# One tick more in a state-space pipeline, one PSUM tile for its inputs and outputs, and weight splits kept in DRAM

## The chip, the cores and the metric

The kernel runs on one core of a Trainium2 chip. The metric is the device time of one execution in microseconds (us), shorter is better. TensorE is PE in the rows (PEld is its weight load), VectorE DVE, ScalarE ACT, GpSimd POOL; SyncE (SP) issues every DMA of this kernel, in program order.

## The reference, cut to what matters

One layer of a hybrid decoder on 2048 prompt tokens (with 16 meta tokens ahead of them) and 8 running sequences of 8 new tokens, model width 1024, all in float32.

```python
xn = rmsnorm(h, norm_gain)
proj = xn @ w_in                       # 1024 x 6144: u_s, z_s, u_p, z_p, gates
# SSM branch: 64 groups of 16 channels, 64 complex states each
s[t] = abar * s[t-1] + bbar @ u_s[t]   # complex recurrence over time
y = gelu(Re(c @ s) + d * u_s)
y_s = y * sigmoid(y @ w_glu + b_glu)
# pooling branch: causal means over windows of 2, 4, 8, 16, then a 256x256 mix
y_p = ((windowed means of u_p) - u_p) @ pool_mix * pool_scale
merged = g_s * ((y_s * silu(z_s)) @ w_branch_ssm) + g_p * ((y_p * silu(z_p)) @ w_branch_pool)
out = rmsnorm(h + merged @ w_out)      # and the new SSM states and pooling rows
```

## The kernel before, in words

Features lie on partitions, tokens on the free axis. Tokens are cut into 4 groups (`GROUPS`, g0 to g3, some 512 to 544 columns each). A **unit** is one 128-row block of one weight matrix (or of the pooling mix) for one group: `proj` runs 8 blocks of depth, and each product of float32 matrices is made of three matmuls (`mm3`, L123): high part of the weight by high part of the data (L128), by its low part (L130), and low part of the weight by the high part (L132). So each weight block is loaded as `raw` (L187), rounded by POOL to `wh` (`w_high`, L103), and its remainder `wl` is taken by DVE (`w_low`, L206). The list `units` fixes the order of all 339 units; PE works through them. In iteration i of the last loop (L1295) the kernel calls `w_high` for unit i+2, then what earlier units left behind (posts), then events, then the matmuls of unit i, and at their end `w_low` for unit i+2 and `w_load` up to five units ahead. Every engine runs its own instructions in the order of the program. `raw`, `wh` and `wl` have 3 buffers each.

The units `us` make the SSM's input `u_s` (8 blocks for each group), in the order g1, g0 at the start, g2 and g3 later; the same 8 weight blocks are loaded and split each time.

The recurrence itself runs for 64 SSM groups in 32 pairs, in two **rounds** over time (`ROUNDS`: 135 and 131 chunks of 8 tokens), as a software pipeline spread over other units by `spread`. In **tick** i the pipeline handles several pairs, each at another step (`EARLY`, `LATE`, L587): the EARLY steps are put into the program a quarter of a tick in, the LATE ones at its end, between matmuls of the unit. For pair q: `st_load` (tick q, LATE) loads the input `su` and a matrix `smb`; `st_x` (q+1, LATE) is the PE product into the PSUM tile `sx`; `st_turn_a` (q+2, EARLY) copies `sx` with ACT (L519, L520; in round 1 also L522, which takes the last columns to `xs`); `st_turn_v` (q+2, EARLY) multiplies `sx` with DVE (L528); `st_scan` (q+2, LATE) is the scan (L540); `st_swap` (q+3, EARLY; L546) and `st_rot` (q+3, LATE) turn it back; `st_state` (q+4, EARLY) makes the state tile `sS` on POOL (L569); `st_y` (q+4, LATE) multiplies on PE into the PSUM tile `sy`, with `su` (L577) and with `sS` (L578); `st_out` (q+5, EARLY) copies `sy` to `sY` with ACT (L582) and stores it to `ys` in DRAM. `sx` and `sy` are two PSUM tiles with one buffer each; `sS` and `sY` have one buffer.

Round 0 has 37 ticks in 34 units (39 to 72: the `brp`/`gp` units of g0, and the `us` units of g2 and g3), so seven units hold two ticks. Round 1 has 37 ticks between units 75 and 217, at most one in a unit.

At the start the weight blocks of units 0 and 1 are loaded and split before the loop (L1267 to L1283); then SP issues the load of block 2 (L1284), some constants, and the rows of x for g0. In iteration 0 POOL first rounds block 2 (L103) and then adds squares of x (`x_sq`, L720), as DVE does; ACT makes the squares in two temporaries, of which each is free again when its sum is done. DVE puts both sums together (L723), and at the start of unit 2 PE sums them over the partitions (L746).

The matrices of the recurrence are made in the background at the start (`batches`) and kept in DRAM in `mat_d`. PSUM tiles that are needed elsewhere: `acc` (2 x 512 columns, 3 buffers) for all units; `bx` and `by`, one half each, for two early sums of squares (`rms_sum`, L746). `rsqrt_mean` reads such a sum with ACT (L137) and then with DVE (L139), one half after the other, into separate columns of its SBUF tiles.

Of the kernel before, what the change touches and what calls it, by code (L numbers as in the profile page):

```python
# [20 lines left out]
P = 128  # L21
# [67 lines left out]
def hybrid_step(ctx, tc, a):  # L89
# [74 lines left out]
    mat_d = dram.tile([GRP, P, 3, P], F32, name="mat_d")  # L164
# [13 lines left out]
    def w_load(key, k=1):  # L178
        if key in raws or key in halves or key in splits:
            return  # L180
# [18 lines left out]
    def w_low(key, k=1):  # L199
# [146 lines left out]
    def batches(bg):  # L346
# [63 lines left out]

        def s5(b):
# [4 lines left out]
            SY.dma_start(mat_d[gs, :, 0].rearrange("g p m -> p g m"), btT)  # L416
            SY.dma_start(mat_d[gs, :, 2].rearrange("g p m -> p g m"), d["ct"].rearrange("p g c t -> p g (c t)"))
# [19 lines left out]
        def s10(b):  # L437
# [5 lines left out]
            SY.dma_start(mat_d[4 * b:4 * b + 4, :, 1].rearrange("g p m -> p g m"), mp)  # L443
# [34 lines left out]
    def st_load(g, q):  # L478
        x = stile("su", 4, g.kn + NS)
# [5 lines left out]
        SY.dma_start(mb, mat_d[two(q), :, 0].rearrange("q p m -> p q m"))  # L485
# [21 lines left out]
    def st_x(g, q):  # L507

        d = pr[q]
        d["px"] = sw["sx"][:, :, :g.kn]  # L510
# [3 lines left out]
    def st_turn_a(g, q):  # L514
# [6 lines left out]
        if g.last:  # L521
            A.activation(sw["xs"][:, two(q)], ps[:, :, kp:], AF.Copy)  # L522
# [20 lines left out]
    def st_swap(g, q):  # L543
# [16 lines left out]
    def st_state(g, q):  # L560
# [3 lines left out]
        s = stile("sS", 1, g.kn)  # L564
# [8 lines left out]
    def st_y(g, q):  # L573
        d = pr[q]
        d["py"] = sw["sy"][:, :, :g.kn]
        for j in range(2):
            PE.matmul(d["py"][:, j], d["m"][:, j, :P], d["u"][:, j], start=True, stop=False)  # L577
            PE.matmul(d["py"][:, j], d["m"][:, j, P:], d["S"][:, j], start=False, stop=True)  # L578
# [18 lines left out]
    def final_states():  # L597
        SY.dma_start(a["fin"], state)
# [815 lines left out]
```

## Time and profile before

| what | value |
|---|---|
| median of 3 runs | 2157.99 us (2157.77 to 2158.32) |
| the profiled execution's own time | 2159.06 us |
| its span | 2157.3 us |
| PE busy | 2086.0 us (97%) |
| DVE, POOL, ACT busy | 1395.2 (65%), 923.7 (43%), 686.8 us (32%) |
| mean granted TensorE clock | 0.989 of full speed |

The span is from the first to the last instruction of the program. Busy time is the time in which at least one instruction of the engine ran; matmuls overlap in the record, so the sum of their durations is more than the busy time. Idle time is put down to what released the engine.

### The profile page before, as it was taken

Reading aid. Unit: us, or ns where it says so; the run is one execution under the profiler, and the core shown is the slowest. Engines: PE = TensorE matmul, PEld = TensorE weight load, DVE = VectorE, ACT = ScalarE, POOL = GpSimd, SP = SyncE. Lnnn points to the kernel's source line nnn. Section 1 sums busy time; section 2 is a strip of 40 time slices with the busy share of each in tenths; the row PEclk is TensorE's granted clock in tenths of the full one; section 3 lists DMA queues with packets and bytes.
Section 4 is the critical chain, followed back from the end, with each engine's and each line's share of the span. In section 5 each row is a group of like instructions: output and inputs, shape, how many; then the busy total and the mean of one; then the engine's idle time right before and its main releaser. Section 6 shows DMA issues by size and latency. Waiting matters only on the chain.

```text
span 2157.3 us, 37693 instructions
## 1 busy us (share of the span) xinstructions
PE 2086.0 (97%) x14968; PEld 1970.9 (91%) x14968; DVE 1395.2 (65%) x1916; ACT 686.8 (32%) x1243; POOL 923.7 (43%) x1054
## 2 busy tenths in 40 slices
PE   7999999889899999999899999999999999999998
PEld 7988899888799999999899999999999987888887
DVE  7989968878656686644856676633633767456444
ACT  3213357645434332144544432121210221112101
POOL 3387747565444452233544452233421333244222
PEclk9999999999999999999999999999999999999999
DMA  6646556486944453244444543234333443343223
GB/s 199 145 117 165 164 169 200 144 202 155 183 127 124 151 144 120 89 121 137 120 125 144 157 139 125 82 119 118 104 100 109 144 128 120 101 133 117 91 97 105
DMA packets 261279, 287.77 MB, mean 133 GB/s; under 512 B 106096, under 2 KB 203760, under 8 KB 261104
## 3 DMA queue, kind: packets, MB, share of 16 engines
q1 hardware_dynamic: 261104, 285.37, 45.7%
q8 instruction: 118, 1.93, 0.4%
q14 instruction: 57, 0.47, 0.1%
HBM read 242.32 MB, written 40.62 MB: 131 GB/s over the span
## 4 chain that ended last, share of the span: by engine, by line
PE 71%; DVE 6%; DMA 4%; ACT 3%; issue 2%; POOL 2%; SPq 0%; DVEq 0%; ACTq 0%; POOLq 0%
PE acc L128 23%; PE acc L132 23%; PE acc L130 23%; DMA ys<-sY 1%; DVE wl L206 1%; DVE sX L537 1%; PE sy L578 1%; PE sx L512 1%; PE sy L577 1%; DVE sX L540 1%; DMA raw<-in_wb 1%; DVE al L114 1%; DVE sph L558 1%; DMA mat_d<-mp 1%; DVE sph L499 0%
## 5 line engine op out<-in xcount | busy, mean ns | idle before, releaser
L128 PE MATMUL acc<-ah,wh 128*128 128x268 f32 (+4 forms) x4504 | 1058.9, 305 | 8.9 <-ACT ah L705 6.6
L132 PE MATMUL acc<-ah,wl 128*128 128x268 f32 (+4 forms) x4504 | 1049.0, 302 | 3.7 <-DVE wl L206 3.7
L130 PE MATMUL acc<-al,wh 128*128 128x268 f32 (+4 forms) x4504 | 1047.9, 302 | 0.0
L103 POOL TENSOR_SCALAR wh<-raw 128x1024 fp32r<-128x1024 f32 (+1 forms) x336 | 392.5, 1168 | 969.9 <-PE acc L130 869.7
L128 PEld LDWEIGHTS acc<-ah,wh 128*128 128x128 f32 x4504 | 729.3, 190 | 44.2 <-issue 7.8
L132 PEld LDWEIGHTS acc<-ah,wl 128*128 128x128 f32 x4504 | 727.8, 189 | 32.0 <-DVE wl L206 4.7
L130 PEld LDWEIGHTS acc<-al,wh 128*128 128x128 f32 x4504 | 728.2, 190 | 27.0 <-DVE al L706 0.3
L206 DVE TENSOR_TENSOR wl<-raw,wh 128x1024 fp32r<-128x1024 f32 (+1 forms) x336 | 432.3, 1288 | 140.9 <-POOL wh L103 136.1
L896 ACT ACTIVATE sg<-acc,hb 128x536 f32<-128x536 f32 (+2 forms) x64 | 45.0, 702 | 402.2 <-PE acc L132 402.1
L528 DVE TENSOR_TENSOR sX<-sx,scc 128x270 f32<-128x270 f32 (+1 forms) x64 | 27.2, 424 | 107.3 <-ACT xs L522 65.0
L114 DVE TENSOR_TENSOR al<-H,ah 128x536 fp32r<-128x536 f32 (+3 forms) x96 | 89.3, 963 | 6.8 <-POOL ah L103 5.2
L952 DVE SCALAR_TENSOR_TENSOR H<-po,H 128x536 f32<-128x536 f32 (+2 forms) x32 | 23.8, 745 | 103.4 <-ACT po L950 103.4
L853 ACT ACTIVATE H<-acc 128x536 f32<-128x536 f32 (+2 forms) x64 | 39.1, 610 | 140.9 <-PE acc L132 140.7
L105 ACT ACTIVATE ah<-H 128x536 fp32r<-128x536 f32 (+3 forms) x80 | 50.8, 646 | 92.6 <-DVE H L884 77.1
L854 DVE SCALAR_TENSOR_TENSOR H<-H,acc 128x536 f32<-128x536 f32 (+2 forms) x64 | 44.8, 700 | 48.1 <-ACT H L853 47.6
L577 PE MATMUL sy<-su,smc 128*128 128x135 f32 (+1 forms) x256 | 52.2, 285 | 18.7 <-ACT sY L582 15.7
L820 DVE TENSOR_TENSOR w<-E 128x483 f32<-128x483 f32 (+2 forms) x32 | 21.9, 685 | 73.4 <-POOL E L807 58.0
L963 DVE SCALAR_TENSOR_TENSOR sg<-sg,acc 128x536 f32<-128x536 f32 (+2 forms) x32 | 22.4, 700 | 70.9 <-PE acc L132 70.9
L540 DVE TENSOR_TENSOR_SCAN sX<-r,state,sX 128x135 f32<-128x135 f32 (+1 forms) x128 | 65.7, 554 | 2.3
L950 ACT ACTIVATE po<-acc,hb 128x536 f32<-128x536 f32 (+2 forms) x32 | 22.5, 704 | 134.8 <-PE acc L132 134.8
L905 DVE SCALAR_TENSOR_TENSOR G<-sg,acc 128x536 f32<-128x536 f32 (+2 forms) x32 | 22.4, 699 | 64.9 <-PE acc L132 64.9
L578 PE MATMUL sy<-sS,smc 128*128 128x135 f32 (+1 forms) x256 | 53.1, 290 | 11.2 <-POOL sS L569 11.2
(232 smaller groups left out, 2227.8 us busy)
## 6 DMA issues: line engine op xcount, KB each, us to landing
raw<-in_wb SPq DMA_DIRECT2D x318, 512.0 KB, 3.8
smc<-mat_d SPq DMA_DIRECT2D x64, 256.0 KB, 4.1
smb<-mat_d SPq DMA_DIRECT2D x64, 128.0 KB, 3.3
xr<-in_xb SPq DMA_DIRECT2D x21, 268.0 KB, 4.4
H<-in_xb SPq DMA_DIRECT2D x19, 268.0 KB, 4.4
su<-us SPq DMA_DIRECT2D x32, 135.0 KB, 4.1
ys<-sY SPq DMA_DIRECT2D x32, 135.0 KB, 4.6
us<-po SPq DMA_DIRECT2D x16, 268.0 KB, 6.6
```

The costliest lines, as they stand in the source:

```text
L103: G.tensor_scalar(out, in_, 1.0, 0.0, ALU.mult, ALU.add)
L105: A.activation(out, in_, AF.Copy)
L114: V.tensor_tensor(l, x, h.bitcast(F32), ALU.subtract)
L128: PE.matmul(out, wh, xh, start=first, stop=False)
L130: PE.matmul(out, wh, xl, start=False, stop=False)
L132: PE.matmul(out, wl, xh, start=False, stop=last)
L206: V.tensor_tensor(l[:, c], r[:, c], h[:, c].bitcast(F32), ALU.subtract)
L540: V.tensor_tensor_scan(x[:, j], r8[:, i].to_broadcast([P, g.kp]), x[:, j], state[:, i], ALU.mult, ALU.add)
L577: PE.matmul(d["py"][:, j], d["m"][:, j, :P], d["u"][:, j], start=True, stop=False)
L578: PE.matmul(d["py"][:, j], d["m"][:, j, P:], d["S"][:, j], start=False, stop=True)
L854: V.scalar_tensor_tensor(self.v3(out), self.v3(out), 1.0, self.pv(ps), ALU.add, ALU.mult)
L896: A.activation(self.v3(s), self.pv(ps), AF.Tanh, scale=0.5, bias=hb[:, b, fb:fb + 1])
```

## The change

- **Weights.** When one of the 8 `us` weight blocks is split for the first time (for g1), its `wh` and `wl` are also stored to DRAM (`wu_d`, 2 x 512 KB). For g2 and g3 the units have kind "v": `w_high` then loads `wh` and `wl` from there, and nothing is loaded as `raw`, rounded or subtracted.
- **Pipeline.** `st_y` comes one tick later (offset 5), `st_out` at 6; the loading of its matrix becomes a step of its own at the end of EARLY (`st_mat`, offset 4). `sx` and `sy` become views of one PSUM tile `bk` of 2 x 512 columns: `sx` of even and odd pairs in the first 320 columns of the two halves, `sy` in columns 320 to 480 of both. `su` has 5 buffers, `sS` 3, and `st_out` writes its output into the pair's `sS`; `sY` is gone. `xs` goes pair by pair to DRAM and is read back in `final_states`. There are 38 ticks to a round.
- **Matrices.** `mat_d` is laid out by pairs, so that rows of the DMAs are twice as long.
- **Pooling.** The windowed sums of `up_post` run over flattened rows where they can, and the small copies of L822 are gone.

```diff
-    mat_d = dram.tile([GRP, P, 3, P], F32, name="mat_d")
+    mat_d = dram.tile([GRP // 2, P, 3, 2, P], F32, name="mat_d")
+    xs_d = dram.tile([P, GRP, NS], F32, name="xs_d")
...
+    wu_d = [dram.tile([P, 2, 1024], F32, name=f"wu{f}") for f in range(NB)]
...
     def w_load(key, k=1):
-        if key in raws or key in halves or key in splits:
+        if key in raws or key in halves or key in splits or key[0] == "v":
...
     def w_high(key, k=1):
...
+        if key[0] == "v":
+            hl = [wpool.tile([P, 1024], F32R, tag=t, bufs=3, name=t) for t in ("wh", "wl")]
+            for j in range(2):
+                SY.dma_start(hl[j].bitcast(F32), wu_d[key[1]][:, j])
+            splits[key] = hl
+            return
...
     def w_low(key, k=1):
...
+        if key[1] < NB and key[0] == "w" and key[1] not in stored:
+            stored.add(key[1])
+            for j, x in enumerate((h, l)):
+                SY.dma_start(wu_d[key[1]][:, j], x.bitcast(F32))
...
     def st_load(g, q):
-        x = stile("su", 4, g.kn + NS)
+        x = stile("su", 5, g.kn + NS)
...
-        SY.dma_start(mb, mat_d[two(q), :, 0].rearrange("q p m -> p q m"))
+        SY.dma_start(mb, mat_d[q, :, 0])
...
     def st_x(g, q):
-        d["px"] = sw["sx"][:, :, :g.kn]
+        d["px"] = sw["sx"][q % 2][:, :2 * g.kn].rearrange("p (q k) -> p q k", q=2)
...
     def st_turn_a(g, q):
         if g.last:
-            A.activation(sw["xs"][:, two(q)], ps[:, :, kp:], AF.Copy)
+            xs = stile("sxs", 2, NS)
+            A.activation(xs, ps[:, :, kp:], AF.Copy)
+            SY.dma_start(xs_d[:, two(q)], xs)
...
+    def st_mat(g, q):
+        d = pr[q]
         d["m"] = stile("smc", 2, 2 * P)
-        SY.dma_start(d["m"].rearrange("p q (j m) -> p q j m", j=2),
-                     mat_d[two(q), :, 1:3].rearrange("q p j m -> p q j m"))
+        SY.dma_start(d["m"], mat_d[q, :, 1:3].rearrange("p j q m -> p j (q m)"))
...
     def st_state(g, q):
-        s = stile("sS", 1, g.kn)
+        s = stile("sS", 3, g.kn)
...
     def st_out(g, q):
-        y = stile("sY", 1, g.kn)
-        A.activation(y, pr.pop(q)["py"], AF.Copy)
+        d = pr.pop(q)
+        y = d["S"]
+        A.activation(y, d["py"], AF.Copy)
         SY.dma_start(chans(g, ys_d, q), y)
...
-    EARLY = ((5, st_out), (3, st_swap), (2, st_turn_a), (1, st_sin), (4, st_state),
-             (0, st_phase), (2, st_turn_v), (2, st_turn_g))
-    LATE = ((3, st_rot), (0, st_wrap), (2, st_scan), (4, st_y), (1, st_x), (0, st_load))
-    NTICK = NPAIR + 5
+    EARLY = ((6, st_out), (3, st_swap), (2, st_turn_a), (1, st_sin), (4, st_state),
+             (0, st_phase), (2, st_turn_v), (2, st_turn_g), (4, st_mat))
+    LATE = ((3, st_rot), (0, st_wrap), (2, st_scan), (5, st_y), (1, st_x), (0, st_load))
+    NTICK = NPAIR + 6
...
     def up_post(self, fb, ps):
                 if d < T:
-                    V.tensor_tensor(nxt[:, d:], cur[:, d:], cur[:, :T - d], ALU.add)
                     V.tensor_tensor(nxt[:, :d, 1:], cur[:, :d, 1:], cur[:, T - d:, :ke - 1], ALU.add)
-                    V.tensor_copy(nxt[:, :d, 0:1], cur[:, :d, 0:1])
...
     def u_us(g, f, delay=2):
-        i = add("w", W_US + f, g.us, f)
+        i = add("v" if g.gi > 1 else "w", W_US + f, g.us, f)
...
     def to_ssm():
-        for n in ("sx", "sy"):
-            sw[n] = ps.tile([P, 2, 160], F32, name=n)
-        sw["xs"] = sw["p"].tile([P, GRP, NS], F32, name="xs")
+        bk = ps.tile([P, 2, 512], F32, name="bk")
+        sw["sx"] = [bk[:, j, :320] for j in range(2)]
+        sw["sy"] = bk[:, :, 320:480]
```

## Rows read from the trace of the kernel before

**Rows 1.** The page: busy time by engine.
```profile
PE 2086.0 (97%) x14968; PEld 1970.9 (91%) x14968; DVE 1395.2 (65%) x1916; ACT 686.8 (32%) x1243; POOL 923.7 (43%) x1054
```

**Rows 2.** Waits of PE over the span: us in total, times, longest.
```profile
PE sy L577 <- ACT sY L582: 15.7, 8, 3.3
PE sy L578 <- POOL sS L569: 11.2, 11, 1.7
PE sx L512 <- DVE sX L528: 10.4, 10, 2.2
PE sy L577 <- DMA smc<-mat_d: 2.9, 3, 1.3
```

**Rows 3.** Windows at the low clock: the last in the pipeline; sum of eight.
```profile
1275.70:1279.10 3.40, 3.40 (x18) 3.40 (x17) 3.05 (x6) 0.00 (x0) 2.25 (x3) 0.50 0.38 91
...
sum 40.80, PE 37.64 PEld 35.54 DVE 31.59 ACT 17.98 POOL 24.16; mean PE 4.71 PEld 4.44 DVE 3.95 ACT 2.25 POOL 3.02
```

**Rows 4.** Groups by line: busy us, mean ns | idle before, releasers.
```profile
L206 DVE TENSOR_TENSOR wl<-raw,wh 128x1024 fp32r<-128x1024 f32 (+1 forms) x336 | 432.3, 1288 | 140.9 <-POOL wh L103 136.1 <-DMA mt<-ks 4.3
...
L528 DVE TENSOR_TENSOR sX<-sx,scc 128x270 f32<-128x270 f32 (+1 forms) x64 | 27.2, 424 | 107.3 <-ACT xs L522 65.0 <-ACT sXw L520 42.3
...
L582 ACT ACTIVATE sY<-sy 128x270 f32<-128x270 f32 (+1 forms) x64 | 24.6, 384 | 36.9 <-DMA ys<-sY 35.1 <-PE sy L578 1.7
...
L822 DVE COPY w<-w 128x2 f32<-128x2 f32 (+1 forms) x40 | 7.4, 185 | 0.0
```

**Rows 5.** Timeline of all engines, one tick of round 1: start, us, instruction.
```profile
1270.61 0.40 PE L132 MATMUL acc<-ah,wl 128*128 128x268 f32 x2
...
1272.59 0.49 PE L577 MATMUL sy<-su,smc 128*128 128x131 f32 x2 [1.58 <-ACT sY L582]
...
1274.40 0.41 DVE L528 TENSOR_TENSOR sX<-sx,scc 128x246 f32<-128x246 f32 x1 [0.44 <-ACT xs L522]
...
1274.71 0.49 PE L578 MATMUL sy<-sS,smc 128*128 128x131 f32 x2 [1.63 <-POOL sS L569]
...
1275.49 0.86 PE L512 MATMUL sx<-su,smb 128*128 128x131 f32 x4
```

**Rows 6.** Timeline, the first tick in which L528 ends after PE's arrival.
```profile
343.43 0.39 PE L577 MATMUL sy<-su,smc 128*128 128x135 f32 x2
...
343.48 0.44 DVE L528 TENSOR_TENSOR sX<-sx,scc 128x270 f32<-128x270 f32 x1 [1.34 <-ACT sXw L520]
```

**Rows 7.** Timeline, ACT and DVE: halves of one PSUM tile read, of two tiles.
```profile
411.67 0.44 DVE L139 SCALAR_TENSOR_TENSOR sg<-acc,sg 128x268 f32<-128x268 f32 x1
...
412.14 0.48 ACT L137 ACTIVATE sg<-acc,epst 128x268 f32<-128x268 f32 x1 [0.98 <-DVE sg L139]
```
**Rows 8.** Timeline, the same lines where the halves are two tiles.
```profile
48.61 0.49 ACT L137 ACTIVATE sg<-by,epst 128x272 f32<-128x272 f32 x1
```

**Rows 9.** Timeline of the start.
```profile
8.20 0.33 SPq L187 DMA_DIRECT2D raw<-in_wb  x1
...
15.10 1.08 POOL L103 TENSOR_SCALAR wh<-raw 128x1024 fp32r<-128x1024 f32 x1 [3.04 <-DMA raw<-in_wb]
15.19 2.06 DVE L206 TENSOR_TENSOR wl<-raw,wh 128x1024 fp32r<-128x1024 f32 x1
...
20.48 1.34 POOL L720 TENSOR_TENSOR ss<-ss,w 128x536 f32<-128x536 f32 x1 [2.04 <-ACT w L719]
...
26.33 1.20 PE L746 MATMUL bx<-rs,onesm 128*128 128x268 f32 x2 [3.32 <-DVE rs L723]
```

**Rows 10.** DMA from 440 to 485 us: share of 16 engines; issues, median us to landing.
```profile
q1 hardware_dynamic: 12506, 9.44, 92.7%
...
raw<-in_wb SPq DMA_DIRECT2D x5, 512.0 KB, 5.4
...
ys<-sY SPq DMA_DIRECT2D x6, 135.0 KB, 5.9
```

**Rows 11.** DMA from 5 to 13 us, where large packets fill the engines.
```profile
DMA packets 1350, 2.85 MB, mean 356 GB/s; under 512 B 147, under 2 KB 248, under 8 KB 1350
```

More of the change, by code (lines that the diff above doesn't have):

```diff
@@ L172, in hybrid_step @@
     raws, halves, splits = {}, {}, {}
+    stored = set()
+    wu_d = [dram.tile([P, 2, 1024], F32, name=f"wu{f}") for f in range(NB)]
     def cut(n, k):
@@ L409, in s4, with mat_store @@
             d["ps"], d["pk"] = ps, pk
+        def mat_store(b, j, x):
+            SY.dma_start(mat_d[2 * b:2 * b + 2, :, j].rearrange("q p g m -> p q (g m)"),
+                         x.rearrange("p (q g) m -> p q (g m)", g=2))
         def s5(b):
@@ L415, in s5 @@
             A.activation(btT, d["ps"], AF.Copy)
-            SY.dma_start(mat_d[gs, :, 0].rearrange("g p m -> p g m"), btT)
-            SY.dma_start(mat_d[gs, :, 2].rearrange("g p m -> p g m"), d["ct"].rearrange("p g c t -> p g (c t)"))
+            mat_store(b, 0, btT)
+            mat_store(b, 2, d["ct"].rearrange("p g c t -> p g (c t)"))
             o = 4 * (b % 2)
@@ L442, in s10 @@
                          mt[:, o:o + 4].rearrange("p g (t c) -> p g c t", c=GCH), AF.Copy)
-            SY.dma_start(mat_d[4 * b:4 * b + 4, :, 1].rearrange("g p m -> p g m"), mp)
+            mat_store(b, 1, mp)
         S7 = [(7 + i, lambda b, i=i: s7(b, i)) for i in range(1, NPART)]
@@ L576, in st_y @@
         for j in range(2):
-            PE.matmul(d["py"][:, j], d["m"][:, j, :P], d["u"][:, j], start=True, stop=False)
-            PE.matmul(d["py"][:, j], d["m"][:, j, P:], d["S"][:, j], start=False, stop=True)
+            m = slice(j * P, (j + 1) * P)
+            PE.matmul(d["py"][:, j], d["m"][:, 0, m], d["u"][:, j], start=True, stop=False)
+            PE.matmul(d["py"][:, j], d["m"][:, 1, m], d["S"][:, j], start=False, stop=True)
     def st_out(g, q):
-        y = stile("sY", 1, g.kn)
-        A.activation(y, pr.pop(q)["py"], AF.Copy)
+        d = pr.pop(q)
+        y = d["S"]
+        A.activation(y, d["py"], AF.Copy)
         SY.dma_start(chans(g, ys_d, q), y)
-    EARLY = ((5, st_out), (3, st_swap), (2, st_turn_a), (1, st_sin), (4, st_state),
-             (0, st_phase), (2, st_turn_v), (2, st_turn_g))
-    LATE = ((3, st_rot), (0, st_wrap), (2, st_scan), (4, st_y), (1, st_x), (0, st_load))
-    NTICK = NPAIR + 5
+    EARLY = ((6, st_out), (3, st_swap), (2, st_turn_a), (1, st_sin), (4, st_state),
+             (0, st_phase), (2, st_turn_v), (2, st_turn_g), (4, st_mat))
+    LATE = ((3, st_rot), (0, st_wrap), (2, st_scan), (5, st_y), (1, st_x), (0, st_load))
+    NTICK = NPAIR + 6
     def tick(steps, g, i):
@@ L598, in final_states @@
         SY.dma_start(a["fin"], state)
+        xs, s0 = (tmp.tile([P, GRP, NS], F32, tag="po", bufs=2, name="s0") for _ in range(2))
+        SY.dma_start(xs, xs_d)
         for j in range(2):
-            s0 = tmp.tile([P, GRP, NS], F32, tag="po", bufs=2, name="s0")
             SY.dma_start(s0, a["s0"][:, j])
             G.tensor_tensor(s0, s0, a8[:, j].unsqueeze(2).to_broadcast([P, GRP, NS]), ALU.mult)
-            G.tensor_tensor(sw["xs"], sw["xs"], s0, ALU.add)
-        SY.dma_start(a["fins"], sw["xs"])
+            G.tensor_tensor(xs, xs, s0, ALU.add)
+        SY.dma_start(a["fins"], xs)
     mid = []
@@ L818, in up_post @@
                 nxt = self.t(tmp, f"w{step % 2}", 1, shape=[P, T, ke])
+                if d < 4:
+                    n, o, c = (x.rearrange("p t k -> p (t k)") for x in (nxt, cur, cur))
+                    i = d * ke + step
+                    V.tensor_tensor(n[:, i:], o[:, i:], c[:, step:T * ke - d * ke], ALU.add)
+                elif d < T:
+                    V.tensor_tensor(nxt[:, d:, 1:], cur[:, d:, 1:], cur[:, :T - d, 1:], ALU.add)
+                else:
+                    V.tensor_tensor(nxt[:, :, 2:], cur[:, :, 2:], cur[:, :, 1:ke - 1], ALU.add)
                 if d < T:
-                    V.tensor_tensor(nxt[:, d:], cur[:, d:], cur[:, :T - d], ALU.add)
                     V.tensor_tensor(nxt[:, :d, 1:], cur[:, :d, 1:], cur[:, T - d:, :ke - 1], ALU.add)
-                    V.tensor_copy(nxt[:, :d, 0:1], cur[:, :d, 0:1])
-                else:
-                    V.tensor_tensor(nxt[:, :, 1:], cur[:, :, 1:], cur[:, :, :ke - 1], ALU.add)
                 cur = nxt
```

## The prediction

> **What bounds the kernel now.** I read the page first. PE is busy in 97% of the span [rows 1], so the change can only be worth what lies in PE's waits, and what it adds to them. The list of PE's waits comes next, since it names what ended each. PE idles for 71 us in all (the span less its busy time), and 40 of these lie in the SSM pipeline [rows 2]: the product y waits for its PSUM tile to be copied out (15.7 us), for the state tile (11.2) and for its matrix (2.9), and the product x waits for DVE to have read `sx` (10.4). The rest lies at the start and in waits for DVE.
>
> Third, the granted clock. There are eight windows at half clock inside the span (1.2 GHz, the lower of the two levels), 40.8 us together [rows 3]. Two of 3.4 us belong to the first 130 us; the other six, 34 us, each follow a tick in which PE stood still for 2.8 us or more. At half clock half of that is lost: 17 us. So a pipeline without waits would give 40 + 17 = 57 us at most. That is what the change could win.
>
> Fourth, the groups by line, for who holds whom. ACT stood 35.1 us in `st_out` until the store of the pair before had left `sY` [rows 4]: that delays everything behind it on ACT, `st_swap` and `st_turn_a` too, and so the DVE multiplication L528. L528 itself waits for ACT, 65.0 us of it for L522. L522 reads other columns of `sx` and writes `xs`, which L528 doesn't touch; both only read. So in this program two engines don't read one PSUM tile at once, whatever the columns: the order of the program is kept by semaphores. The timeline of two sums of squares tells more. Where both halves lie in one `acc` tile, ACT's read of the second half starts at 412.14, 0.03 us after DVE's read of the first half (411.67 + 0.44), after a wait of 0.98 us [rows 7]; the same holds at 817, 1299 and 1742 us. Where the halves are two tiles, `bx` and `by`, it doesn't wait at all [rows 8]. So the waits go by tile, and not by half.
>
> **The pipeline, part by part.** What goes: `st_y` a tick later has its state tile ready, so PE's 11.2 us for POOL go. With `sY` gone, ACT no longer waits for the store in `st_out` (35.1 us of ACT). The wait moves to POOL: `sS` with 3 buffers comes free when that same store has landed, again a tick after its issue, so `st_state` waits in its place, and behind it on POOL `st_phase`, `st_turn_g` and the next rounding. That has a tick of slack before PE needs it, and I cost it at nothing; without the slack it is again the 11.2 us.
>
> What comes: `sx` and `sy` lie in one tile now. In the program of one tick the accesses are: `st_out` (ACT), `st_turn_a` (ACT), `st_turn_v` (DVE, L528), `st_y` and `st_x` (PE). By [rows 4, 7] `st_y` must therefore wait for L528 of the same tick, which it didn't before. Before, only `st_x` did, and the 8 instructions of `st_y` ran ahead of it (the last six of them take 0.78 us in [rows 5], so all 8 about 1 us). So two tiles for x buy nothing, since y stands in front of x in PE's order. A tick of round 1 shows it [rows 5]: PE is through with the unit at 1271.0, y starts at 1272.59 and goes on at 1274.71, x at 1275.49. L528 ends at 1274.81. Then y could begin only there: 3.8 us of waiting in place of 3.2.
>
> I go through all 64 ticks in this way. In 27 of them L528 ends after PE arrived at y; the first is that of [rows 6] (343.92 against 343.43), the last that of [rows 5]. The sum is 60.3 us, against 39.7 us of PE waits in the same ticks. From the 60.3 I take 10 us for ticks of round 0 in which ACT had waited for the store (where, instead, the scan of the tick before or DVE's own queue sets the end); 3.8 us and 2.2 us at the first waiting tick of round 1 and the last of round 0, where y and L528 no longer meet because of the tick more; and 2 us for ticks in which DVE was late and has 1.29 us less to do per `us` unit [rows 4]. I add 1.8 us, since the 38 ticks of round 1 fall on other units: three instead of two in the `zs` units of g1, where ACT is late. That is 60.3 - 10 - 3.8 - 2.2 - 2 + 1.8 = 44.1 us against 39.7: **+4.4 us**. The bounds: if y waits only for `st_out`, some 15 us remain (-25); if POOL's new wait is late for PE too, the 11.2 us come back, +16.
>
> The matrix load `st_mat` is issued as long before its product as it was, a tick and three quarters; on SP it now stands behind the store of `xs` (round 1), which waits for L522, 2 us of ACT after the `st_out` that it stood behind before. It has ticks of 12 us there: 0, at most the 2.9 us of [rows 2] once more.
>
> Clock: seven or eight ticks would have a wait of 2.8 us or more in one piece, against six windows now: **+2 us**, between -12 and +8.
>
> By the Trainium skill (PSUM — Partial Sum Buffer, "PSUM bank collisions raise a hardware error") two engines must be kept apart by bank, reads against reads included, and different banks may be used at the same time. By that rule the sum would be 6 us less, as in the second rival below. The trace agrees on reads against reads (L522 and L528), and not on the banks: the rows at 412 us hold back the other half of the tile too.
>
> **The weights.** For 16 units POOL loses a rounding and DVE a subtraction [rows 4]; neither holds PE in those units except as counted. In their place SP loads 1 MB a unit instead of 0.5 MB, after PE has left the slot of the unit before, with two units of time until it is needed. Behind that wait on SP stand the loads of x, the stores to `ys` and the loads of `su` of the same unit; none of them could be used before PE is there either, so the order costs nothing, only the bytes do. But from 440 to 485 us, in the `us` units of g2, the DMA engines are 92.7% busy, and a store of 135 KB takes 5.9 us to land [rows 10]. Large packets go at 356 GB/s when the engines are full [rows 11], so 512 KB cost 1.5 us of all engines, for 6 units of that stretch 9 us; the free share is 3.3 us, and the longer rows of `mat_d` give back something that no row prices. So up to 5 us don't fit there; in the units of g3 less, since the stretch is not full. I take **+5 us**, bounds 0 (the work slides into idle stretches beside it) and +18 (16 units by 1.5 us are 24 us, of which a quarter finds room).
>
> **The start.** Here is a term that I can follow exactly. Each first split now issues two stores from SP, in the place of `w_low`. For block 1 that lies ahead of the load of block 2, and waits for DVE's subtraction, which comes after all of `x_raw` and ends at 17.25 [rows 9]. Before, the load of block 2 was issued at 8.20 and POOL rounded it at 15.10. Now it is issued at about 17 (the subtraction a little faster without POOL beside it) and lands behind a 512 KB store: some 4.5 us later, at 21 to 22.5. POOL stands at the rounding until then, and its adds of squares stand behind it; ACT's squares wait for them in turn. From 22 on: rounding 1.1, three adds of 1.34 [rows 9] with two squares of 0.65 between them, DVE's sum 1.0 to 1.5: 29 to 31. PE's sum L746 starts there and not at 26.33. PE has nothing else: **+3.5 us**, bounds +2.5 and +6 (a longer stretch at the low clock). The stores hold their `wh` and `wl` until they have landed, but these slots are used again three units later. The other six pairs of stores fall on weights that are loaded three units ahead: 0.
>
> **The rest.** 72 small copies go, 7.4 us of DVE for the larger group [rows 4]. PE waits for DVE in two places of the pooling units of g0; I take **-1 us**, bounds 0 and -3. `final_states` now uses one tile for two loads in turn: SP stands there for some us longer, but PE does not wait at all there in this trace; 0, at most +3. The 32 small stores of `xs` cost SP a place behind ACT in round 1, where loads have more than a tick; 0.
>
> Sum: 4.4 + 2 + 5 + 3.5 - 1 = +13.9 us on 2159.06 us of the profiled execution, 2173.0 us. That execution was 1.07 us above the median, so I predict 2172 us.
>
> **Rivals.** What a measurement can tell from no change is 0.2%, 4.3 us.
> - *Faster, 2129 us.* Views of one tile are kept apart by what they touch. Then x has two places and y waits for `st_out` alone: 25 us of waits and 12 us of clock go, the start, the DMA and the copies keep 7.5. For it: the three largest waits of [rows 2] are those that the change addresses. Against it: L522 and L528, and the rows at 412 us. It decides if PE no longer waits for L528. 0.15.
> - *By halves, 2166 us* (2160 to 2172). y's half goes ahead of L528 where the pair's `sx` lies in the other half: every second one of some 25 waiting ticks, 12 by 0.5 us. For it: the halves are 512 columns each, as those of `acc`. Against it: [rows 7]. This is the page's rule. 0.14.
> - *The DMA engines become the bound, 2191 us.* 18 us in place of 5, and 8 us of clock in place of 2: PE waits for `su`, `smc` and x. For it: 92.7%. Against it: the stretches beside it have room. 0.15.
> - *Nothing, 2158 us.* ACT's 35 us had hidden more than I credit, and that just pays for the start. 0.06.
>
> My forecast (2162 to 2182) has 0.50. The range 2145 to 2192 leaves out nearly all of the first rival and a third of the third. Chances: faster 0.18 (the first rival, and half of the last), same 0.14 (the other half, the lower edge of the second rival and of my own case), slower 0.68.
>
> **What would show it.** Among PE's waits, that of L578 for POOL is gone, and the largest is y (L577) for DVE's L528, 35 to 45 us; there is none of x for L528. ACT's wait for the store is gone, POOL has one. L746 starts at 29 to 31 us. DMA landings in the `us` units grow to 6 to 8 us. If y starts while L528 still reads, the forecast is wrong; if L746 starts before 28, the start is.

## The result, and the profile after

The changed kernel takes 2188.89 us (median of 4 runs, 2185.74 to 2189.65) against 2158.15 us of the kernel before beside it: 1.0138 times as long (95% interval 1.0122 to 1.0154), 30.7 us more. The forecast was 2172 us: slower is right and the time lies in the range, but the loss is more than double the 13.9 us that the sum had. The profiled execution took 2189.61 us, its span is 2187.8 us, the mean granted clock 0.982. All line numbers below are those of the kernel that a fence names. The new names of the lines that matter, for the changed kernel: y with `su` L577 is L600, with `sS` L578 is L601, x L512 is L530, DVE's multiplication L528 is L548, `st_out` L582 is L606, the sum L746 is L771, the copy of `u_s` L770 is L795.

The page's busy time of the changed kernel (compare [rows 1]):

```profile
PE 2094.1 (96%) x14968; PEld 1980.4 (91%) x14968; DVE 1352.4 (62%) x1828; ACT 686.4 (31%) x1243; POOL 899.3 (41%) x1038
```

Its list of PE's waits (us in total, times, longest; compare [rows 2]):

```profile
PE bk L600 <- DVE sX L548: 35.8, 15, 5.1
PE bx L771 <- DVE rs L748: 13.0, 2, 8.2
PE bk L600 <- DMA smc<-mat_d: 11.2, 4, 4.3
...
PE acc L128 <- DVE po L795: 5.3, 1, 5.3
PE bk L530 <- DVE sX L548: 4.8, 3, 3.6
```

Two numbers split the loss. PE's matmuls are the same 14968, so I put the 8.1 us that its busy time grew down to the clock. Its idle time grew from 71.3 to 93.7 us (span less busy), by 22.4. Together that is 30.5 us, the difference of the two spans. The largest wait is the one that the forecast named, and it has the size that the forecast gave it (35 to 45 us). PE's wait for POOL's `sS` is gone, ACT's for the store too: it went to POOL (58.9 us). No wait of PE names POOL there, but one of them comes of it, as the rows at 511 us below show. Groups by line of the changed kernel (busy us, mean ns | idle before, releasers; compare [rows 4]):

```profile
L548 DVE TENSOR_TENSOR sX<-bk,scc 128x270 f32<-128x270 f32 (+1 forms) x64 | 27.1, 424 | 111.4 <-ACT sxs L541 61.7 <-ACT sXw L538 49.7
L606 ACT ACTIVATE sS<-bk 128x270 f32<-128x270 f32 (+1 forms) x64 | 24.5, 383 | 26.2 <-PE bk L530 20.7 <-PE bk L601 3.8 <-POOL state L592 1.6
L590 POOL COPY sS<-state 128x2 f32<-128x2 f32 x64 | 23.7, 370 | 60.1 <-DMA ys<-sS 58.9 <-PE bk L601 1.1
```

The tick of [rows 5] again, in the timeline of the changed kernel (start, us, instruction):

```profile
1305.34 0.41 DVE L548 TENSOR_TENSOR sX<-bk,scc 128x246 f32<-128x246 f32 x1 [0.44 <-ACT sxs L541]
...
1305.81 0.49 PE L600 MATMUL bk<-su,smc 128*128 128x131 f32 x2 [3.40 <-DVE sX L548]
```

The same timeline, in a tick of round 1 that has x but no y yet:

```profile
684.94 0.40 DVE L548 TENSOR_TENSOR sX<-bk,scc 128x246 f32<-128x246 f32 x1
...
685.40 0.75 PE L530 MATMUL bk<-su,smb 128*128 128x131 f32 x4 [3.65 <-DVE sX L548]
```

Before, the tick's wait was in two pieces, 1.58 and 1.63 us, with a product of y between them; now it is one piece of 3.40. The row at 685.40 rules out the rival by halves: x writes the half of `bk` that L548 does not read, and waits for L548 all the same, 3.65 us.

The windows at the low clock, as in [rows 3] (start and end, length, then busy us and instructions of PE, PEld, DVE, ACT and POOL, the granted clock, the DMA share and GB/s; three of the 15 inside the span, and the sum):

```profile
27.20:34.00 6.80, 3.10 (x10) 2.66 (x11) 4.72 (x6) 2.57 (x4) 3.09 (x2) 0.50 1.02 371
54.50:61.30 6.80, 5.17 (x19) 4.71 (x20) 6.35 (x21) 0.97 (x2) 0.00 (x0) 0.50 0.27 82
...
508.50:515.30 6.80, 4.10 (x19) 4.13 (x20) 6.66 (x11) 0.79 (x1) 2.04 (x2) 0.50 0.55 168
...
sum 71.40, PE 60.22 PEld 58.21 DVE 61.85 ACT 20.60 POOL 31.45; mean PE 4.01 PEld 3.88 DVE 4.12 ACT 1.37 POOL 2.10
```

15 windows and 71.4 us, where there were eight and 40.8. The window at 508.50 begins in the wait for L795, whose chain stands in the timeline:

```profile
504.04 0.19 POOL L590 COPY sS<-state 128x2 f32<-128x2 f32 x1 [6.60 <-DMA ys<-sS]
...
506.36 0.89 DVE L517 SCALAR_TENSOR_TENSOR sph<-scc,sph 128x272 f32<-128x272 f32 x1 [3.08 <-POOL scc L511]
...
510.35 0.70 DVE L795 TENSOR_TENSOR po<-acc,rs 128x536 f32<-128x536 f32 x1
...
511.20 0.78 PE L128 MATMUL acc<-ah,wh 128*128 128x264 f32 x2 [5.33 <-DVE po L795]
```

POOL stands 6.60 us for the store of `ys` in `st_state`, so its L511 of the next step comes late, DVE waits 3.08 us for that, and L795, which frees the `acc` tile for PE, stands behind it in DVE's order. The start, in the timeline of the changed kernel (compare [rows 9]):

```profile
15.97 0.32 SPq L220 DMA_DIRECT2D wu<-wl  x1
16.34 0.42 SPq L191 DMA_DIRECT2D raw<-in_wb  x1
...
22.00 1.05 POOL L103 TENSOR_SCALAR wh<-raw 128x1024 fp32r<-128x1024 f32 x1 [9.87 <-DMA raw<-in_wb]
...
30.90 1.26 PE L771 MATMUL bx<-rs,onesm 128*128 128x268 f32 x2 [8.24 <-DVE rs L748]
...
48.82 0.72 DVE L795 TENSOR_TENSOR po<-acc,rs 128x536 f32<-128x536 f32 x1 [2.72 <-DMA us<-po]
...
56.13 1.27 PE L771 MATMUL bx<-rs,onesm 128*128 128x272 f32 x2 [4.78 <-DVE rs L748]
```

The first sum comes at 30.90, as forecast (29 to 31): the load of block 2 is issued behind the store of block 1 and POOL stands until 22.00. But PE's second sum of squares is late as well: 56.13, where it began at 47.38 before. Last, the DMA from 440 to 485 us (compare [rows 10]; issues, KB each, median us to landing):

```profile
q1 hardware_dynamic: 10947, 12.07, 99.8%
...
wh<-wu SPq DMA_DIRECT2D x4, 512.0 KB, 6.0
wl<-wu SPq DMA_DIRECT2D x4, 512.0 KB, 7.4
...
us<-po SPq DMA_DIRECT2D x4, 268.0 KB, 8.3
```

### The profile page after: what moved, and what is told of

Its sections match the earlier page's. It is cut to its first block, busy times and chain, and to the rows that moved or that the text cites. A ratio compares the mean times of both kernels' runs of the same rounds, so it can differ in the third digit from the quotient of the medians.

```text
span 2187.8 us, 37748 instructions
## 1 busy us (share of the span) xinstructions
PE 2094.1 (96%) x14968; PEld 1980.4 (91%) x14968; DVE 1352.4 (62%) x1828; ACT 686.4 (31%) x1243; POOL 899.3 (41%) x1038
## 4 chain that ended last, share of the span: by engine, by line
PE 67%; DVE 6%; DMA 5%; ACT 3%; POOL 3%; issue 2%; SPq 1%; DVEq 0%; POOLq 0%; ACTq 0%
PE acc L128 22%; PE acc L132 22%; PE acc L130 22%; DMA ys<-sS 2%; DVE wl L216 1%; DVE sX L557 1%; PE bk L600 1%; DMA us<-po 1%; DMA mat_d<-mp 1%; PE bk L601 1%; DVE al L114 1%; PE bk L530 1%; DVE sX L560 1%; DMA H<-in_xb 1%; POOL sS L591 1%
## 5 line engine op out<-in xcount | busy, mean ns | idle before, releaser
L128 PE MATMUL acc<-ah,wh 128*128 128x268 f32 (+4 forms) x4504 | 1063.0, 306 | 15.3 <-POOL wh L103 6.0
L103 POOL TENSOR_SCALAR wh<-raw 128x1024 fp32r<-128x1024 f32 (+1 forms) x320 | 370.8, 1159 | 959.5 <-PE acc L130 888.4
L132 PEld LDWEIGHTS acc<-ah,wl 128*128 128x128 f32 x4504 | 729.6, 190 | 30.5 <-DVE wl L216 3.2
L216 DVE TENSOR_TENSOR wl<-raw,wh 128x1024 fp32r<-128x1024 f32 (+1 forms) x320 | 414.8, 1298 | 158.7 <-POOL wh L103 157.9
L600 PE MATMUL bk<-su,smc 128*128 128x135 f32 (+1 forms) x256 | 56.2, 303 | 47.2 <-DVE sX L548 35.8
L548 DVE TENSOR_TENSOR sX<-bk,scc 128x270 f32<-128x270 f32 (+1 forms) x64 | 27.1, 424 | 111.4 <-ACT sxs L541 61.7
L600 PEld LDWEIGHTS bk<-su,smc 128*128 128x128 f32 x256 | 42.1, 203 | 53.4 <-DVE sX L548 40.1
L935 DVE SCALAR_TENSOR_TENSOR G<-sg,acc 128x536 f32<-128x536 f32 (+2 forms) x32 | 22.4, 700 | 71.2 <-PE acc L132 71.2
L993 DVE SCALAR_TENSOR_TENSOR sg<-sg,acc 128x536 f32<-128x536 f32 (+2 forms) x32 | 22.4, 701 | 71.1 <-PE acc L132 71.1
L560 DVE TENSOR_TENSOR_SCAN sX<-r,state,sX 128x135 f32<-128x135 f32 (+1 forms) x128 | 61.0, 517 | 2.3
```

The lines of the kernel that those rows point to most:

```text
L103: G.tensor_scalar(out, in_, 1.0, 0.0, ALU.mult, ALU.add)
L128: PE.matmul(out, wh, xh, start=first, stop=False)
L132: PE.matmul(out, wl, xh, start=False, stop=last)
L560: V.tensor_tensor_scan(x[:, j], r8[:, i].to_broadcast([P, g.kp]), x[:, j], state[:, i], ALU.mult, ALU.add)
L600: PE.matmul(d["py"][:, j], d["m"][:, 0, m], d["u"][:, j], start=True, stop=False)
```

## The experiments

The theory after the result: the weights cost at the start and through the DMA engines; the one PSUM tile, held as a whole, costs through y's wait and the clock. The rivals: the tile costs nothing of itself (DVE is late anyway), the order on SP costs and not the bytes, the tick more costs by itself. Ratios are to the kernel before, run beside each.

### Which part costs what

**e1_two_tiles**: the changed kernel with two PSUM tiles.

```diff
-        bk = ps.tile([P, 2, 512], F32, name="bk")
-        sw["sx"] = [bk[:, j, :320] for j in range(2)]
-        sw["sy"] = bk[:, :, 320:480]
+        for n in ("sx", "sy"):
+            sw[n] = ps.tile([P, 2, 160], F32, name=n)
```

> The changed kernel with the input and the output of the pipeline in two PSUM tiles again (one buffer each, as before the change), all else as changed. If the tile that is held as a whole is what costs the pipeline: y waits no longer for DVE's multiplication (35.8 us of waits in the changed kernel), x waits for it instead, some 10 to 13 us as before, and PE's 11.2 us for POOL and most of the 15.7 us for ACT stay away thanks to the tick more: 2170 us (2163 to 2178). If what holds y is only that DVE is late and the queues of DMA are full, x waits as long as y did and the time stays at 2184 to 2189 us.

Measured: 2179.18 us, 1.0095 (1.0080 to 1.0110), between the two ranges. y no longer waits for DVE and x does (16.9 us), but y waits 12.6 us for its matrix and 15.8 for ACT.

**e2_no_store**: the changed kernel without splits in DRAM.

```diff
-        i = add("v" if g.gi > 1 else "w", W_US + f, g.us, f)
+        i = add("w", W_US + f, g.us, f)
...
-                SY.dma_start(wu_d[key[1]][:, j], x.bitcast(F32))
```

> The changed kernel without the splits kept in DRAM: no stores, and groups 2 and 3 load, round and subtract the input projection as before. The one PSUM tile stays. If the weights cost their 9.8 us at the start and some 10 us more through full DMA queues in round 0: 2169 us (2163 to 2174), PE's first two sums of squares at 26 and 47 us, and the largest wait still y for DVE's multiplication, 30 to 40 us. If the weights cost only the start: 2179 us.

Measured: 2171.03 us, 1.0059 (1.0044 to 1.0074), in the first range; the first two sums of squares are at 26.43 and 48.78 us.

**e3_no_store_two_tiles**: both edits.

> Both undone: no splits kept in DRAM, and two PSUM tiles with one buffer each. What is left is the tick more, the state tile that also takes the output, the matrices by pairs and the pooling without its small copies. If tile and weights are two costs that add: 2150 us (2140 to 2160), below the kernel before, with 10 to 13 us of waits of x for DVE and next to none of y. If the tick more gains nothing of itself: 2155 to 2160 us.

Measured: 2163.24 us, 1.0020 (1.0011 to 1.0029), above both.

**e4_weights_only**: the kernel before with the weights' part of the change and nothing else.

> The kernel before with the weights' part alone: splits stored once, loaded again for groups 2 and 3. If this part costs 9.8 us at the start and 9 to 12 us in round 0: 2177 us (2170 to 2182). If the full queues only hurt together with the other parts: 2168 us. The forecast had put it at 8.5 us, 2167 us.

Measured: 2172.87 us, 1.0069 (1.0052 to 1.0086), in the first range.

What follows: the weights cost 0.0079 of the time beside the one tile (1.0138 less 1.0059), 0.0075 beside two tiles, 0.0069 alone: 15 to 17 us. The one tile costs 0.0043 with the splits and 0.0039 without: 8 to 9 us. Some 4 us are left with the rest (e3), which was to gain. Since the parts add, the rival that they hurt only together falls. The waits of PE, first in the list of e2:

```profile
PE bk L596 <- DVE sX L544: 32.5, 15, 4.3
...
PE bk L526 <- DVE sX L544: 3.7, 1, 3.7
PE bk L596 <- ACT sS L602: 2.9, 1, 2.9
PE bk L596 <- DMA smc<-mat_d: 2.8, 2, 1.9
...
PE bk L526 <- DMA smb<-mat_d: 2.4, 2, 1.5
```

The list of e3:

```profile
PE sx L526 <- DVE sX L544: 15.6, 14, 3.7
PE sy L596 <- ACT sS L602: 12.3, 6, 4.7
PE sy L596 <- DMA smc<-mat_d: 11.1, 5, 4.5
...
PE acc L128 <- DVE po L791: 4.0, 1, 4.0
```

In e3 the waits in the pipeline come to 40.3 us (with 1.3 for `smb`, not shown), where the kernel before had 41.2 (40.2 in [rows 2], and 1.0 for `smb`): POOL's 11.2 us are gone and y's for ACT are 3.4 less, and x's wait for DVE and y's for its matrix have grown by 13.4. So the 4 us that e3 loses don't lie in the pipeline's waits: its idle time is 74.7 us, 3.4 more than before, and the wait for L791 (the copy of `u_s`) alone has grown by 3.6; its busy time is 1.9 us longer. In e2 the pipeline's waits come to 44.3, 4.0 more than in e3. A tick of round 1 in the timeline of e3, with two pieces of waiting:

```profile
1032.41 0.49 PE L596 MATMUL sy<-su,smc 128*128 128x131 f32 x2 [1.16 <-ACT sS L602]
...
1034.69 0.72 PE L526 MATMUL sx<-su,smb 128*128 128x131 f32 x4 [1.11 <-DVE sX L544]
```

The same tick in e2, with one:

```profile
1036.34 0.81 PE L596 MATMUL bk<-su,smc 128*128 128x131 f32 x2 [3.44 <-DVE sX L544]
```

The one wait is longer than the two together (3.44 against 2.27 us), since y's eight matmuls no longer fill the time until L544 ends. In e2 a window at the low clock begins in this wait, and the two matmuls behind it take 0.81 us in place of 0.49; in e3 there is none at this tick. That doesn't hold tick by tick: in the last tick of this kind e3 has two pieces (1.14 us at 1279.16, 1.11 at 1281.43) and e2 one (3.42 at 1290.00), and a window of 3.40 us follows in both, as it did both before and after the change in the tick of [rows 5]. The windows at the low clock inside the span, that one and the sum, in e2:

```profile
1035.30:1042.10 6.80, 5.76 (x26) 5.76 (x27) 6.19 (x10) 4.95 (x8) 3.68 (x7) 0.50 0.36 88
...
sum 64.70, PE 58.11 PEld 56.81 DVE 53.86 ACT 26.05 POOL 30.62; mean PE 4.47 PEld 4.37 DVE 4.14 ACT 2.00 POOL 2.36
```

The sum in e3:

```profile
sum 51.30, PE 46.04 PEld 44.88 DVE 39.80 ACT 18.70 POOL 20.60; mean PE 4.19 PEld 4.08 DVE 3.62 ACT 1.70 POOL 1.87
```

PE is busy 2093.0 us in e2 and 2087.9 in e3: 5.1 us of the tile's 8 to 9 I put down to the clock. The changed kernel and e1 are a second such pair: 2094.1 and 2088.7 us busy, 71.4 and 58.1 us at the low clock. So with one tile there are 13.3 and 13.4 us more of the low clock, and 5.4 and 5.1 us more of busy time.

### The start and the bytes

**e5_store_later**: e4 with the stores at the second split.

```diff
-        if key[1] < NB and key[0] == "w" and key[1] not in stored:
-            stored.add(key[1])
+        new = key[1] < NB and key[0] == "w" and key[1] not in stored
+        stored.add(key[1] if key[0] == "w" else -1)
+        if key[1] < NB and key[0] == "w" and (key[1] == NB - 1) == new:
```

> The kernel before with the weights' part alone, but with the stores of the splits moved from the first split (for g1) to the second (for g0); only block 7, which is split once for both, is stored at its first split. If the start loses because the stores stand on SP ahead of the load of block 2 and share the DMA engines with the tiles of x and u_s that PE's first sums need: the 10 us of the start go, PE's first two sums of squares are at 26 and 47 us again, and 2163 us (2160 to 2166) is left, the share of round 0. If the stores cost the same bytes wherever they are: 2172 us, as without the move.

Measured: 2163.93 us, 1.0029 (1.0018 to 1.0040), in the first range.

**e10_store_from_2**: the same with `(key[1] > 1) == new` in the last line, so that only blocks 0 and 1 are stored later.

> The weights' part alone (2173 us), with only the stores of blocks 0 and 1 moved to their second split; blocks 2 to 7 are stored at their first split as in the change. If the first sum of squares is late because the load of block 2 stands behind the stores of blocks 0 and 1 on SP, and the second because the stores of the later blocks share the DMA engines with the tiles of u_s: the first sum is at 26 us again, the second stays some 5 us late, and the time is 2167 to 2169 us. If one delay is only the follower of the other: 2164 us, as with all stores moved.

Measured: 2168.32 us, 1.0040 (1.0027 to 1.0054), in the first range.

The second sum of squares in the timeline of e4:

```profile
55.80 0.86 PE L757 MATMUL bx<-rs,onesm 128*128 128x272 f32 x2 [3.40 <-DVE rs L734]
```

In that of e10:

```profile
50.51 1.28 PE L758 MATMUL bx<-rs,onesm 128*128 128x272 f32 x2 [4.64 <-DVE rs L735]
```

In that of e5:

```profile
48.39 0.97 PE L758 MATMUL bx<-rs,onesm 128*128 128x272 f32 x2 [3.38 <-DVE rs L735]
```

The first sum is at 31.41 in e4, 26.91 in e10 and 26.04 in e5. So storing blocks 0 and 1 later brings the first sum back by 4.5 us, and the second by 5.3; storing the others later brings the second back by 2.1 more. The stores at the start cost 0.0040 (e4 less e5, each known to some 0.001 to 0.002), some 8.6 us, and the times of e10 and e5 overlap, so that only the trace tells those two apart. What is left in e5, 0.0029 or 6.3 us, is the loading in round 0.

**e6_bytes_only**: the kernel before with 512 KB more moved in each of the 16 units.

```diff
+        seen[key] = seen.get(key, 0) + 1
+        if key[0] == "w" and key[1] < NB and seen[key] > 1 + (key[1] < NB - 1):
+            SY.dma_start(dm_d, a["wb"][key[1]])
```

> The kernel before with an additional copy of 512 KB from DRAM to DRAM in each of the 16 us units of groups 2 and 3, issued where the changed kernel issues its loads; nothing waits for it, and rounding and subtraction stay. If it is the bytes that make round 0 longer: 2163 to 2167 us, with landings of 7 to 10 us in the us units. If it is the order on SP (the loads of wh and wl wait for PE's slot, and x, us and ys stand behind them): 2158 to 2160 us.

Measured: 2168.77 us, 1.0055 (1.0038 to 1.0072), above the first range. Bytes for which nothing waits cost as much as the loads do, or more (the copy is read from DRAM and written to DRAM, so it moves more than the loads add). So bytes alone can cost this much, and the order on SP isn't needed to explain the loss; that the order adds something of its own is not excluded. PE's wait for `smc` in e6 is 11.4 us, against 2.9 before, and y's for ACT 10.0 against 15.7.

### What the tick more does

**e7_own_output**: e3 with `sS` in 2 buffers and an `sY` of its own.

```diff
-        s = stile("sS", 3, g.kn)
+        s = stile("sS", 2, g.kn)
...
-        y = d["S"]
+        y = stile("sY", 1, g.kn)
```

> The kernel with the tick more, two PSUM tiles and no splits in DRAM (2163 us), with an output tile of its own again: two state tiles and one output tile in place of three shared ones. POOL no longer waits 46.6 us for the stores, ACT does, some 30 us. If POOL's wait delays the next pair's rotation and so DVE and x: 2158 us (2156 to 2160), waits of x for DVE under 12 us. If only the larger count of slow-clock windows and ACT's place behind the gelu steps matter: 2162 to 2165 us, or later where ACT waits for the store.

Measured: 2164.67 us, 1.0035 (1.0024 to 1.0046). POOL's wait is gone, ACT waits 41.2 us for the store in its place, and nothing is won. PE's wait for L791 is there again (4.5 us), this time behind ACT: `st_out` at 494.32 stands 5.08 us for the store, the multiplication L544 at 496.44 stands 4.09 for ACT, L791 comes at 501.31. A kernel in which neither waits was not tried.

**e8_mats_pooling**: the kernel before with the matrices by pairs and the new pooling alone.

> The kernel before with two parts of the change alone: the matrices kept by pairs and the pooling without its small copies. The forecast put the pooling at 1 us less and the matrices at nothing: 2155 to 2158 us against some 2157. If what the tick more seemed to cost (4 us without the splits and with two tiles) belongs to these parts instead: 2160 to 2162 us.

Measured: 2158.22 us, 0.9999 (0.9990 to 1.0008): nothing, either way. So e3's 4 us belong to the part of the change that is called Pipeline: by the rows, to the wait for L791 and the clock.

**e9_by_bank**: e2 with two tiles of 512 columns, x ahead of y.

```diff
-        bk = ps.tile([P, 2, 512], F32, name="bk")
-        sw["sx"] = [bk[:, j, :320] for j in range(2)]
-        sw["sy"] = bk[:, :, 320:480]
+        bk = [ps.tile([P, 512], F32, name=f"bk{j}") for j in range(2)]
+        sw["sx"] = [bk[j][:, :320] for j in range(2)]
+        sw["sy"] = [bk[j][:, 320:480] for j in range(2)]
...
-    LATE = ((3, st_rot), (0, st_wrap), (2, st_scan), (5, st_y), (1, st_x), (0, st_load))
+    LATE = ((3, st_rot), (0, st_wrap), (2, st_scan), (1, st_x), (5, st_y), (0, st_load))
```

> The changed kernel without splits in DRAM (2171 us), with the one PSUM tile cut into two tiles of 512 columns: x of even pairs lies in the first, of odd pairs in the second, y by halves in both; x is issued ahead of y, and y's half in the free tile ahead of the other. If a tile is held as a whole, x now runs beside DVE's multiplication and so does half of y; only the last four of y's matmuls wait: some 1 us less in each of 18 ticks, and less of the low clock: 2152 to 2160 us, and waits for DVE under 20 us instead of 36. If tiles are not what holds PE, 2168 to 2173 us.

Measured: 2159.55 us, 1.0010 (1.0001 to 1.0020). The tick of 1032 to 1036 us again, in the timeline of e9:

```profile
1029.78 0.39 PE L597 MATMUL bk<-sS,smc 128*128 128x131 f32 x2
1030.80 0.42 DVE L544 TENSOR_TENSOR sX<-bk,scc 128x246 f32<-128x246 f32 x1 [2.79 <-ACT sxs L537]
1031.27 0.81 PE L596 MATMUL bk<-su,smc 128*128 128x131 f32 x2 [1.10 <-DVE sX L544]
```

x (at 1029.00) and y's free half are done ahead of L544, and only the other half waits, 1.10 us. Cutting the tile in two and letting x go first took some 10 us off (1.0059 to 1.0010) though DVE is as late (L544 ends 3.4 us after PE is through with the unit, in e2 and in e9), so the rival that the tile costs nothing falls. No run made only one of the two edits of e9. The Trainium skill (PSUM — Partial Sum Buffer, "PSUM bank collisions raise a hardware error") has engines kept apart by bank, with different banks free at the same time. In e9 the two tiles of 512 columns are used side by side, as that has it; in the changed kernel the program held the tile of 2 x 512 columns as one, 3.65 us in the row at 685.40.

**e11_x_between**: e9 with x between the halves of y, and the load of `smb` moved to the end of EARLY.

```diff
         for j in (q % 2, (q + 1) % 2):
+            if j != q % 2 and q + 4 < NPAIR:
+                st_x(g, q + 4)
...
-             (0, st_phase), (2, st_turn_v), (2, st_turn_g), (4, st_mat))
-    LATE = ((3, st_rot), (0, st_wrap), (2, st_scan), (1, st_x), (5, st_y), (0, st_load))
+             (0, st_phase), (2, st_turn_v), (2, st_turn_g), (4, st_mat), (0, st_mb))
+    LATE = ((3, st_rot), (0, st_wrap), (2, st_scan), (1, st_x0), (5, st_y), (0, st_load))
```

(`st_mb` is the load of `smb`, taken out of `st_load`; `st_x0` issues x for the first four pairs, which have no y beside them.)

> The kernel with a tile for each 512 columns and no splits in DRAM (2159.6 us, 1.0010 of the kernel before), with y's half in the free tile issued first, then x, then y's other half, and the load of x's matrix smb issued at the end of EARLY, three quarters of a tick sooner. There PE waited 12.1 us for smb: half a us in each of 8 ticks for y's half, and smb no longer lands last: 2154 us (2151 to 2157), 2 to 4 us less than the kernel before. If su, which is loaded just ahead of smb, is then as late: 2158 to 2160 us.

Measured: 2161.55 us, 1.0013 (1.0004 to 1.0023), above both: `smb` is no longer late, `smc` and ACT are.

**e12_mended**: e11 with splits in DRAM, stored as in e5.

> The whole change with its two costs mended: a tile for each 512 columns with x between the halves of y, and the splits stored at the second split. If the start and the tile as a whole are what the forecast mis-sized, only the bytes of round 0 (some 7 us) are left above the kernel without splits: 2161 us (2158 to 2166), 28 us less than the changed kernel. If the full queues of round 0 now make smb and su late: 2168 to 2172 us.

Measured: 2170.41 us, 1.0050 (1.0036 to 1.0064), in the second range, 0.0037 or 8 us above e11. But `su` is waited for only 0.9 us and `smb` not at all: PE's idle time is 6.3 us more than in e11, spread over several waits, and its busy time 3.6.

**e13_mat_sooner** and **e14_two_tiles_mat**: e11 and e3 with `st_mat` moved forward; the diff is that of e13.

```diff
-             (0, st_phase), (2, st_turn_v), (2, st_turn_g), (4, st_mat), (0, st_mb))
+             (0, st_phase), (2, st_turn_v), (2, st_turn_g), (0, st_mb))
...
-    LATE = ((3, st_rot), (0, st_wrap), (2, st_scan), (1, st_x0), (5, st_y), (0, st_load))
+    LATE = ((3, st_rot), (0, st_wrap), (2, st_scan), (1, st_x0), (5, st_y), (3, st_mat), (0, st_load))
```

> As the kernel with x between the halves of y (1.0013 of the kernel before), with the load of y's matrix smc moved from the end of EARLY to LATE of the tick before, right behind the y that frees its place: a quarter of a tick sooner, and ahead of the store of ys on SP. If the tick more gains nothing only because the loads now land last (13.6 us of waits for smc): some 10 us of waits and a few us of the low clock go, 2150 us (2146 to 2154), faster than the kernel before. If the engines of DMA are simply full then, another load takes smc's place as the last: 2157 to 2161 us.

> The kernel with the tick more, two PSUM tiles and no splits in DRAM (1.0020 of the kernel before), with the same earlier load of smc. If its 11.1 us of waits for smc are what eats the gain of the tick more: 2152 us (2149 to 2156). If x's wait for DVE (15.6 us) and y's for ACT (12.3 us) then grow by as much, since they run beside it: 2159 to 2163 us.

Measured: e13 2160.48 us, 1.0007 (0.9998 to 1.0016); e14 2162.67 us, 1.0020 (1.0011 to 1.0028). PE's largest waits in the pipeline, in the list of e9:

```profile
PE bk L526 <- DMA smb<-mat_d: 12.1, 8, 3.5
PE bk L596 <- DVE sX L544: 8.8, 10, 1.4
```

In that of e11:

```profile
PE bk L605 <- DMA smc<-mat_d: 13.6, 7, 3.2
PE bk L605 <- ACT sS L612: 11.1, 8, 1.8
```

In that of e13:

```profile
PE bk L605 <- ACT sS L612: 14.9, 9, 3.4
PE bk L533 <- DMA su<-us: 10.5, 7, 4.1
```

Each time that the last load is brought forward, another one or ACT takes its place: with x first it is `smb`, with y first `smc`, with `smc` sooner `su`. My first expectations of 2154 and 2150 us each took one wait away and put nothing in its place. Still, all waits of y and x together are 34.5 us in e9 and 34.8 in e13, some 6.5 less than the 41.2 of the kernel before. What takes most of it back is the wait for the copy of `u_s`: 4.6 and 4.5 us in place of 0.4; in e13 PE's busy time is 4.9 us longer too. No version ran faster than the kernel before.

## Why the prediction was wrong

By its own terms, with what the two traces and the runs show in their place:

- **The pipeline, +4.4 us.** The mechanism was right: y waits for L548 of its tick (35.8 us), and PE's waits for POOL and ACT there are gone. Without the splits (e2) the waits of y and x are 44.3 us, 3.1 more than before; the forecast had +4.4. One statement failed: x does wait for L548, in ticks without a y ahead of it (4.8 us). The rival "faster" falls with the rows at 685 and 1305 us.
- **The clock, +2 us.** This step failed: PE's busy time grew by 8.1 us, the upper bound. The count held: I expected seven or eight waits of 2.8 us or more for L548, and there are eight, seven of them with a window behind them. The price did not: the one tile is worth 5.4 us of busy time (against e1) and 5.1 (e2 against e3). The other 2.7 us I put down to waits that the term left out: the windows at 27.20 and 54.50 begin in those for the first two sums, 508.50 in that for L795, and two of 3.40 us follow waits of 4.30 and 4.32 us for `smc`. Nor is half of a window its cost, as I had it: the 30.6 us more of the low clock would then be 15.3.
- **The weights, +5 us.** Right in size: 6.3 us (e5), or 8 (e12 against e11), and bytes alone can do it (e6). In the changed kernel it shows as y's wait for `smc`, 11.2 us in place of 2.9 (2.8 in e2, without the splits); with two tiles that row doesn't measure it, as e3 without the splits has 11.1. The stretch of 92.7% became one of 99.8%.
- **The start, +3.5 us, at most +6.** This step failed too. The delay of the first sum is 4.6 us (30.90 against 26.33), near what I worked out; but I followed only that sum, and wrote that the other six pairs of stores cost 0 because their slots are not needed soon. The delay grew to 8.8 us at the second sum (56.13 against 47.38). By e10 the larger part of that is still the stores of blocks 0 and 1 (5.3 us), and 2.1 the other six: stores stand among the stores of `us`, whose buffers DVE waits for (48.82, 2.72 us), and behind DVE stand the sums of squares. PE's waits for these two sums are 13.0 us, against 3.8 before; e4 and e5 put the stores of the start at 8.6 us.
- **The rest, -1 us.** The copies gave nothing (e8). In their place came a wait that I had not looked for: at 511.20 us PE stands 5.33 us for DVE's L795. It is there in e1, e2, e3, e7, e9 and e11 to e14 (4.0 to 5.7 us), but not in those that leave the number of ticks as it was, where it is 0.5 us or less. With 38 ticks the last `us` unit of g2 holds two of them, with 37 the one before it: two L548 (497.06 and 502.15) stand between the L795 at 496.44 and the one at 510.35, where the kernel before has one L528 (494.35) between its copies at 492.62 and 498.13. (Its two, at 478.19 and 486.66, stand one copy earlier, and PE doesn't wait for that copy.) That this placing makes PE wait is argued from these rows, and no run moved it. In the changed kernel POOL's wait for the store has a part in it, the 3.08 us at 506.36; so that wait, which I had put at nothing, was not free.

Idle time adds up: 10.6 us in the pipeline (51.8 against 41.2, `smb` included), 9.2 at L771, 4.9 at L795, and 2.3 less elsewhere make 22.4; with 8.1 of clock, 30.5. The three failed terms are 6.1 of clock, 5.7 at the start and 5.9 in the rest too little, 17.7 together, against the 16.6 us by which the sum was short. DMA as the bound (2191 us) was near in time but not in cause: of the 30.5 us, 8.3 are y's longer wait for `smc`. That the time lies in the range at all is luck: its upper end was there for this rival.

That the tick more gains nothing holds as far as e3, e7, e9, e11, e13 and e14 go: without the splits, with two tiles or one for each 512 columns, with the store's wait on POOL or ACT, and with the matrix sooner, the time is 1.0007 to 1.0035 of the kernel before. In the pipeline PE then waits for ACT, DVE or whichever load lands last, and outside it for the copy of `u_s`. Whether 38 ticks that are placed without this last wait would gain is open.

## What to carry to other kernels

Two buffers in one tile are one buffer to the program's semaphores: give each its own tile, and put what can run early ahead in the engine's order. A merged wait is not the sum of its pieces: of one tick, 1.16 and 1.11 us became 3.44, since the work between them came to stand behind. A wait that moves to an engine off the critical path is to be followed further: POOL's came back to PE through DVE. And a store that nobody waits for still costs when it stands on the queue ahead of the first loads: the same stores, issued a group later, cost 8.6 us less.

## What the runs showed of the hardware

- Copies that nobody waits for (e6) lengthened the kernel by 0.55%: from 440 to 485 us loads of `smc` took 7.0 us to land and stores of `us` 7.5 (6.1 and 6.9 before), and PE's wait for `smc` went from 2.9 to 11.4 us. The engines' busy share in that stretch was no higher for it, 90.3% against 92.7%.
- Of one tick, the two waits of 1.16 and 1.11 us in e3 (1032.41 and 1034.69) and the one of 3.44 us in e2 (1036.34) lie around the same work; behind the long one y's first two matmuls took 0.81 us, not 0.49. In e9 the same tick has waits of 1.19 and 1.10 us (1029.00 and 1031.27), and there the low clock did come (a window of 3.40 us from 1030.90).
